# w_out split by column halves and projected during mLSTM's last chunks, x in two transfers a block, the first feed-forward sums beside the projection

## Chip, cores and metric

One core of one Trainium2 chip. The metric is the device time of one execution in microseconds (us), the median of several runs. The profile is of one execution; its times are counted from the start of its span.

## What is computed

One layer of a bidirectional encoder over two groups of positions (2048 and 256, 2304 in all, width 1024), in float32. An mLSTM head group and an attention head group work on the same normed input, their outputs are projected by `w_out` and added to x, and a feed-forward part with a depthwise convolution of width 3 follows.

```python
h = rmsnorm(x, norm1_w); p = h @ w_in
m_out = mlstm_mixer(mq, mk, mv, mo, gates, b_gates, mh_norm_w)      # 8 heads of 64, both directions
a_out = attention_mixer(aq, ak, av, q_norm_w, k_norm_w)             # 8 heads, 2 key/value heads, no mask
x = x + jnp.concatenate([m_out, a_out], axis=-1) @ w_out            # (2304,1024) @ (1024,1024)
h = rmsnorm(x, norm2_w)
u = centred_dwconv(h @ w_up, conv_w, conv_b); a, g = jnp.split(u, 2, axis=-1)
x = x + (jax.nn.silu(g) * a) @ w_down
y = rmsnorm(x, final_norm_w)
```

## The kernel before

Every float32 product is made of three matmuls in a faster format: each operand is split into a rounded high part (ScalarE, ACT, a copy) and the rest (VectorE, DVE, a subtraction), and high x high, high x low and low x high are added up in PSUM. `split` (L109 to L117) loads a piece of a weight into a staging tile and splits it; `loads` in `phase_c` does the same with the mixed heads.

The stages are: phase A (first norm, attention's projections, gates), then mLSTM and attention together, then the projection by `w_out` (`phase_c`), then the feed-forward part (`phase_d`).

mLSTM goes in four pairs of heads over 9 blocks of 256 positions and 18 chunks of 128; in the last pair `proj_qo` makes a block's queries and gates just ahead of its chunks (`out_steps`). A chunk runs through stages in steps (`out_a`, `out_b`, `out_c`, `out_n`, `out_d`), and `out_d` writes it to `mix_d` (L937). Attention goes in 36 head blocks: for each, the row maxima are found first (px, L574, and its reduction on DVE, L575), then for eight pairs of key tiles scores (ps, L600 and L601), two exponentials on ACT (L604, L605), a subtraction on DVE (pl, L606) and six matmuls by the values (pv, L618). The division at the end of a head block takes four reciprocals (L635), and GpSimd (POOL) multiplies and stores into `mix_d`.

Two generators, one for mLSTM and one for attention, yield estimated costs in us, and `run_both` (L1490 and following) decides whose next step is emitted: mLSTM's count `dm` over its total `nm` is held at 1.3 times attention's share. mLSTM's chunk steps carry a high priority (`MPRI`). When mLSTM's generator ends, its pools are closed, `phase_c` is opened, and from there the order of instructions on TensorE (PE) is that of the program (`manual_schedule`), while the other engines and DMA queues are ordered by a planner that simulates times. Now attention's steps alternate with those of `phase_c`: each attention step adds its cost times `pace` to an account, and when the account covers the cost that `phase_c` has yielded, its next step is emitted. A step with a need also waits until that block of attention's output has been emitted.

```python
        pace = C_ALL / (g.a_total - da)
        while da is not None:
            while have >= cost and (need is None or need in g.mixed):
                have -= cost
                need, cost = next(c)
```

`phase_c` first loads and splits `w_out` in 16 pieces of 128 rows by 512 columns (`weights`): rows 0 to 511 into the slots of mLSTM's weights (tag `w`, 8 slots, staged through 2 tiles of `m_r`), rows 512 to 1023 into a pool `wo` that opens when mLSTM's pools are closed, staged through the tiles for x. Then come nine blocks of 256 positions, the last two swapped. A block has four column groups z of 256 output columns; z 0 and 1 read columns 0 to 511 of `w_out`, z 2 and 3 the rest. A column group is 48 matmuls (L1043) into one of two PSUM tiles po, with a yield after each 12 (`C_MM`). `post` adds x to it (L1049), stores the sum to `x1_d` (L1050) and squares it (L1052); POOL adds up the squares (L1054). `tail_a` and `tail_b` make the second norm in the next block's first two column groups: `tail_b` scales (L1064) and stores to `n2_d` (L1066). The next block's `loads` are issued at z = 1. x has eight tiles of [128, 2, 256], two blocks' worth, and a block loads it in eight transfers (L1034).

The feed-forward part multiplies by a Strassen-like scheme with sums of quarters of its input. For the first block of 772 positions `n2_sums` loads rows of `n2_d`, makes four differences on POOL (L1146) and stores them to `n2t_d` (L1148); `n2_load` brings the operands in and splits them (L1125 to L1127); `up_start` loads two rows of `w_up` (L1158, L1159), splits them (L1171, L1172) and starts their matmuls (L1175). After attention's end the rest of `phase_c` is emitted with one of these seven pieces (two loads, four sums, one load) behind each step.

## Time and profile before

| | us |
|---|---|
| median of 3 runs | 3461.38 (3457.83 to 3462.74) |
| the profiled execution | 3460.48 |
| its span | 3458.8 |
| PE busy | 3342.0 (97%) |
| DVE busy | 2683.1 (78%) |
| ACT busy | 1931.2 (56%) |
| POOL busy | 1119.7 (32%) |

The page cuts the span into 40 slices of 86.5 us and gives each engine's busy share in tenths, and the clock that TensorE was granted. A group of instructions is shown with its line, engine, operation, out<-in names and shape, its count, busy time and mean length, and after the bar the idle time of its engine just before it with what ended it. In the timeline a row is the start, the length, the engine, the line and the operation, and in brackets the idle time before it. Matmuls overlap in a full stream, so their lengths add up to more than the time they take: the step from one start to the next is what counts. SPq is the queue from which most transfers are issued, in order.

### The profile page before, as it was taken

The numbers are of one execution on the slowest core, as the hardware profiler recorded it, in microseconds if no ns is written. First come the engines' busy times: TensorE is split into PE (matmuls) and PEld (weight loads), VectorE is DVE, ScalarE is ACT, GpSimd is POOL, SyncE is SP. The second block draws the span as 40 slices with busy tenths as digits, with TensorE's granted clock in tenths as the row PEclk, the third lists the DMA queues.
The fourth block names the chain that finished last, engine by engine and source line by source line (L and its number), as shares of the span: only waits on it lengthen the run. The fifth ranks groups of instructions, "written<-read, shape, count | busy, mean of one in ns | idle before, by whom it ended". The sixth has DMA issues, their size and how long they took to land. (4 is left out here: it accounts for less than half of the span.)

```text
span 3458.8 us, 55780 instructions
## 1 busy us (share of the span) xinstructions
PE 3342.0 (97%) x20058; PEld 3101.0 (90%) x20058; DVE 2683.1 (78%) x4654; ACT 1931.2 (56%) x4329; POOL 1119.7 (32%) x1328
## 2 busy tenths in 40 slices
PE   7989999999999999899998999999999999999998
PEld 6778888888888888678898999999999999999998
DVE  6885687787778788866656888888888878878776
ACT  4536666667666766654444544446544446555555
POOL 6653132213333323201135233225333224322222
PEclk9999999999999999899999999999999999999999
DMA  6765343343345445412348223213433123421221
GB/s 221 237 203 156 91 136 94 105 126 99 111 147 152 126 124 155 131 34 90 98 143 292 74 93 102 74 60 129 135 105 105 62 74 123 142 73 57 74 74 50
DMA packets 258501, 404.29 MB, mean 117 GB/s; under 512 B 33552, under 2 KB 158256, under 8 KB 258224
## 3 DMA queue, kind: packets, MB, share of 16 engines
q1 hardware_dynamic: 230320, 358.24, 32.3%
q0 software_dynamic: 11344, 33.04, 3.5%
q10 hardware_dynamic: 16560, 9.44, 0.9%
q8 instruction: 158, 2.59, 0.3%
q14 instruction: 119, 0.97, 0.1%
HBM read 316.73 MB, written 83.90 MB: 116 GB/s over the span
## 5 line engine op out<-in xcount | busy, mean ns | idle before, releaser
L1313 PE MATMUL pd<-act,wd 128*128 128x384 f32 (+1 forms) x3120 | 594.2, 336 | 18.7 <-DVE acc L1315 11.4
L1313 PEld LDWEIGHTS pd<-act,wd 128*128 128x128 f32 x3120 | 541.0, 189 | 27.0 <-DVE acc L1315 16.6
L606 DVE TENSOR_TENSOR pl<-ps,ph 128x512 fp32r<-128x512 f32 x520 | 353.9, 684 | 205.6 <-ACT ps L605 202.0
L604 ACT ACTIVATE ph<-ps 128x512 fp32r<-128x512 f32 x520 | 309.6, 595 | 261.1 <-PE ps L601 255.1
L1175 PE MATMUL pa<-nt,wut 128*128 128x386 f32 (+2 forms) x2376 | 453.8, 339 | 0.0
L1175 PEld LDWEIGHTS pa<-nt,wut 128*128 128x128 f32 x2376 | 421.0, 189 | 0.0
L575 DVE TENSOR_REDUCE mx<-px 128x1 f32<-128x512 f32 (+1 forms) x528 | 345.0, 671 | 62.5 <-PE px L574 60.5
L1269 DVE SCALAR_TENSOR_TENSOR y<-u,cw,y 128x768 f32<-128x768 f32 (+1 forms) x264 | 311.6, 1181 | 36.2 <-ACT y L1262 29.3
L1180 POOL TENSOR_TENSOR tw<-ru 128x512 f32<-128x512 f32 x66 | 96.0, 1454 | 742.9 <-DMA ru<-w_up 603.6
L618 PE MATMUL pv<-ph,v 128*128 128x512 f32 (+1 forms) x1040 | 323.2, 403 | 2.4 <-ACT ph L604 2.0
L605 ACT ACTIVATE ps<-ps 128x512 f32<-128x512 f32 x520 | 310.6, 597 | 0.0
L1315 DVE TENSOR_TENSOR acc<-pd,acc 128x384 f32<-128x384 f32 (+1 forms) x544 | 280.8, 537 | 32.3 <-PE pd L1313 31.3
L1191 ACT ACTIVATE u<-pa 128x386 f32<-128x386 f32 (+2 forms) x264 | 128.3, 486 | 317.8 <-PE pa L1175 315.7
L574 PE MATMUL px<-kk,qq 128*128 128x512 f32 (+1 forms) x528 | 208.4, 420 | 18.5 <-DVE mx L575 13.4
L1043 PEld LDWEIGHTS po<-cmx,wo 128*128 128x128 f32 x1728 | 217.5, 191 | 7.3
L1043 PE MATMUL po<-cmx,wo 128*128 128x256 f32 x1728 | 220.4, 282 | 0.0
L600 PE MATMUL ps<-qq,kk 128*128 128x512 f32 x520 | 216.4, 418 | 2.9 <-DVE mx L575 1.6
L601 PE MATMUL ps<-qm,kl 65*128 65x512 f32 x520 | 207.4, 401 | 1.3 <-ACT qm L591 1.3
L764 PE MATMUL mj<-mn,wm 128*128 128x256 f32 x1296 | 202.8, 288 | 3.3 <-ACT og L778 1.9
L764 PEld LDWEIGHTS mj<-mn,wm 128*128 128x128 f32 x1296 | 187.0, 192 | 20.4 <-ACT og L778 2.0
L774 PEld LDWEIGHTS mv<-wm,mn 128*128 128x128 f32 x1296 | 182.7, 190 | 18.5 <-ACT qb L770 2.5
L774 PE MATMUL mv<-wm,mn 128*128 128x256 f32 x1296 | 196.4, 285 | 1.0 <-ACT qb L770 0.9
(288 smaller groups left out, 7290.2 us busy)
## 6 DMA issues: line engine op xcount, KB each, us to landing
ru<-w_up SPq DMA_DIRECT2D x132, 512.0 KB, 3.3
mn<-n_d SPq DMA_DIRECT2D x216, 256.0 KB, 3.3
rd<-w_down SPq DMA_DIRECT2D x66, 512.0 KB, 3.6
n_d<-n1T SPq DMA_DIRECT2D x18, 1024.0 KB, 5.6
dm<-nm_d POOLq DMA_DIRECT2D x72, 256.0 KB, 4.1
mjn<-n_d SPq DMA_DIRECT2D x72, 256.0 KB, 3.2
mvn<-n_d SPq DMA_DIRECT2D x72, 256.0 KB, 3.2
q_d<-qz SPq DMA_DIRECT2D x18, 512.0 KB, 3.4
```

The source lines that it names most:

```text
L575: nc.vector.tensor_reduce(s.mx[:, t, z0:z0 + 1], ps[:, 0:w], AX.X, ALU.max)
L604: nc.scalar.activation(ph, ps, AF.Exp)
L605: nc.scalar.activation(ps, ps, AF.Exp)
L606: nc.vector.tensor_tensor(pl, ps, f32(ph), ALU.subtract)
L618: nc.tensor.matmul(s.pv[0:HD if k in (1, 3) else P, 0:N], v, p, start=(kp == 0 and k == 0), stop=(2 * kp + 2 == s.nk and k == 5))
L764: nc.tensor.matmul(pj[:, o], s.w[c][:, a, o * P:(o + 1) * P], nT[c][:, :, h, :], start=(c + o + k == 0), stop=(c == NCC - 1 and k == 2 and ...
L774: nc.tensor.matmul(pv[:, o], nT[c][:, o, a, :], s.w[c][:, h, 256:512], start=(c + o + k == 0), stop=(c == NCC - 1 and k == 2 and o == 1))
L1043: nc.tensor.matmul(po[:, o], wo[c][z // 2][:, a, n], mx[c][:, h, :], start=(c == 0 and k == 0), stop=(c == NCC - 1 and k == 2))
L1175: nc.tensor.matmul(p, w[:, aa, c, :], ops[k][:, c, bb, 0:n], start=c == 0 and i == 0 and not add, stop=c == NCC // 2 - 1 and i == 2, skip_ ...
L1269: nc.vector.scalar_tensor_tensor(y[:, s:e], u[:, s + k:e + k], cw[:, k, jj:jj + 1], y[:, s:e], ALU.mult, ALU.add)
L1313: nc.tensor.matmul(po, wds[j][c // 4][:, aa, c % 4 * P:(c % 4 + 1) * P], acts[j][:, bb, z0:z1], start=(j == 0 and k == 0), stop=(j == len( ...
L1315: nc.vector.tensor_tensor(accs[c][:, z0:z1], po, accs[c][:, z0:z1], ALU.add)
```

## The change

The pieces of `w_out` are taken by column halves: the eight pieces of columns 0 to 511 go into mLSTM's weight slots, the eight of columns 512 to 1023 into the pool `wo`, staged four at a time through two tiles that have the size of a block of x and its tag. All 16 are emitted at once, without yields between them, and the block of the first `loads` is no longer waited for. One lead of 12 stands for the two of 6 and the eight steps of 0.8. In `run_both`, mLSTM's steps are emitted without attention's between them once its count has passed `nm` less 16 (`M_END`). `C_ALL` goes from 178 to 172, and attention's maxima are spread over one pair more of the head block before (`MXZ` 2 to 1).

x is one tile for a block, with two such tiles, loaded in two transfers; the sums are stored in two transfers a block and the normed block in two.

The four `n2_sums` of the first feed-forward block follow `post` in the sixth block of the projection, with tiles of `phase_c`'s pool (tag `rn`, 2 tiles). After attention's end the first two rows of `w_up` are loaded ahead of everything (`up_load`), and the three `n2_load` pieces follow the first three steps.

```diff
-CX = 8
-NPC = 1
-WSTEP = 2
-CSTEP = 1
-C_W = 0.8
-C_LEAD = 6.0
-C_ALL = 178.0
-MXZ = 2
-TP = 4
+C_LEAD = 12.0
+C_ALL = 172.0
+M_END = 16
+MXZ = 1
...
-    def weights(c):
-        wo.append([wps[c // 4].tile([P, 2, 512], F32R, tag="w", name=f"wo{c}_{k}", bufs=WB) for k in range(2)])
-        for k, w in enumerate(wo[c]):
-            if c < 4:
-                t = g.raw.tile([P, 512], F32, tag="raw", name=f"ro{c}_{k}", bufs=2)
-            else:
-                t = sp.tile([P, 512], F32, tag="x", name=f"ro{c}_{k}", bufs=CX)
-            split(g, w[:, 0, :], w[:, 1, :], g.w_out[0, c * P:c * P + P, 512 * k:512 * k + 512], t)
+    def weights(k, c):
+        w = wps[k].tile([P, 2, 512], F32R, tag="w", name=f"wo{c}_{k}", bufs=WB)
+        wo[k].append(w)
+        if k == 0:
+            t = g.raw.tile([P, 512], F32, tag="raw", name=f"ro{c}_{k}", bufs=2)
+        else:
+            if c % 4 == 0:
+                stage.append(sp.tile([P, 4, 512], F32, tag="x", name=f"ro{c}_{k}", bufs=2))
+            t = stage[-1][:, c % 4]
+        split(g, w[:, 0, :], w[:, 1, :], g.w_out[0, c * P:c * P + P, 512 * k:512 * k + 512], t)
...
-        x = [sp.tile([P, 2, BT], F32, tag="x", name=f"cx{b}_{z}", bufs=CX) for z in range(4)]
+        x = sp.tile([P, NCC, BT], F32, tag="x", name=f"cx{b}", bufs=2)
...
-        for z in range(4):
-            for t in range(2):
-                nc.sync.dma_start(x[z][:, :, t * P:(t + 1) * P], g.xT[2 * b + t, :, 2 * z:2 * z + 2])
+        for t in range(2):
+            nc.sync.dma_start(x[:, :, t * P:(t + 1) * P], g.xT[2 * b + t])
...
-        nc.vector.tensor_tensor(x[z], po, x[z], ALU.add)
-        g.st.dma_start(g.x1_d[b, :, 2 * z:2 * z + 2], x[z])
+        xz = x[:, 2 * z:2 * z + 2]
+        nc.vector.tensor_tensor(xz, po, xz, ALU.add)
+        if z % 2:
+            g.st.dma_start(g.x1_d[b, :, 2 * z - 2:2 * z + 2], x[:, 2 * z - 2:2 * z + 2])
...
+            if z % 4 == 3:
+                g.st.dma_start(g.n2_d[:, z - 3:z + 1, b * BT:(b + 1) * BT], x[:, z - 3:z + 1])
...
-    for c in range(NCC):
-        weights(c)
-        yield None, C_W
+    for k in range(2):
+        for c in range(NCC):
+            weights(k, c)
+    sums = list(range(NCC // 2))
     order = (*range(NB - 2), NB - 1, NB - 2)
-    yield 0, C_LEAD
     nxt = loads(0, 0)
     yield None, C_LEAD
...
             post(b, z, x, po, acc)
+            if n > 4 and sums:
+                n2_sums(g, sp, 0, sums.pop(0), tag="rn", bufs=2)
...
-            todo = [lambda c=c: n2_sums(g, s1, 0, c) for c in range(NCC // 2)]
-            todo[TP:TP] = [lambda k=k: n2_load(g, ops, 0, k) for k in EARLY[:2]]
-            todo += [lambda: n2_load(g, ops, 0, EARLY[2])]
+            rs = up_load(g, s1, 0, NFC)
+            todo = [lambda k=k: n2_load(g, ops, 0, k) for k in EARLY]
             for _ in rest:
-                if todo and g.normed >= {t // BT for t in range(DT[1])}:
-                    for f in todo[0:NPC]:
-                        f()
-                    todo = todo[NPC:]
+                if todo:
+                    todo.pop(0)()
...
-            if da is None or dm * g.a_total < LEAD * da * nm:
+            if da is None or dm > nm - M_END or dm * g.a_total < LEAD * da * nm:
```

More of the change, by code (lines that the diff above doesn't have):

```diff
@@ L1004, in phase_c @@
     nc = g.nc
-    wo = []
+    wo = ([], [])
+    stage = []
     g.normed = set()
-    def weights(c):
-        wo.append([wps[c // 4].tile([P, 2, 512], F32R, tag="w", name=f"wo{c}_{k}", bufs=WB) for k in range(2)])
-        for k, w in enumerate(wo[c]):
-            if c < 4:
-                t = g.raw.tile([P, 512], F32, tag="raw", name=f"ro{c}_{k}", bufs=2)
-            else:
-                t = sp.tile([P, 512], F32, tag="x", name=f"ro{c}_{k}", bufs=CX)
-            split(g, w[:, 0, :], w[:, 1, :], g.w_out[0, c * P:c * P + P, 512 * k:512 * k + 512], t)
+    def weights(k, c):
[8 more added lines that the diff above has]
+        split(g, w[:, 0, :], w[:, 1, :], g.w_out[0, c * P:c * P + P, 512 * k:512 * k + 512], t)
     def loads(n, b):
         mx = []
-        x = [sp.tile([P, 2, BT], F32, tag="x", name=f"cx{b}_{z}", bufs=CX) for z in range(4)]
+        x = sp.tile([P, NCC, BT], F32, tag="x", name=f"cx{b}", bufs=2)
         for z in range(4):
@@ L1042, in mm @@
                 for k, (a, h) in enumerate(((0, 0), (0, 1), (1, 0))):
-                    nc.tensor.matmul(po[:, o], wo[c][z // 2][:, a, n], mx[c][:, h, :],
+                    nc.tensor.matmul(po[:, o], wo[z // 2][c][:, a, n], mx[c][:, h, :],
                                      start=(c == 0 and k == 0), stop=(c == NCC - 1 and k == 2))
@@ L1061, in tail_b @@
         r = rstd_rows(g, ps, r, BT)
-        for z in range(4):
-            for o in range(2):
-                nc.vector.scalar_tensor_tensor(x[z][:, o], x[z][:, o], g.n2w[:, 2 * z + o:2 * z + o + 1],
-                                               r, ALU.mult, ALU.mult)
-            g.st.dma_start(g.n2_d[:, 2 * z:2 * z + 2, b * BT:(b + 1) * BT], x[z])
+        for z in range(NCC):
+            nc.vector.scalar_tensor_tensor(x[:, z], x[:, z], g.n2w[:, z:z + 1], r, ALU.mult, ALU.mult)
+            if z % 4 == 3:
+                g.st.dma_start(g.n2_d[:, z - 3:z + 1, b * BT:(b + 1) * BT], x[:, z - 3:z + 1])
         g.normed.add(b)
-    for c in range(NCC):
-        weights(c)
-        yield None, C_W
+    for k in range(2):
+        for c in range(NCC):
+            weights(k, c)
+    sums = list(range(NCC // 2))
     order = (*range(NB - 2), NB - 1, NB - 2)
-    yield 0, C_LEAD
     nxt = loads(0, 0)
@@ L1131, with n2_sums @@
 SUMS = {"t1": (0, 0), "t3": (0, 1), "t4": (1, 0), "t2": (1, 1)}
-def n2_sums(g, pool, b, c, engs=("gpsimd",) * 4):
+def n2_sums(g, pool, b, c, engs=("gpsimd",) * 4, tag="raw", bufs=RW):
     nc = g.nc
@@ L1140, in n2_sums @@
     for k in range(2):
-        r = pool.tile([P, D], F32, tag="raw", name=f"rn{b}_{c}_{k}", bufs=RW)[:, 0:2 * n].rearrange("p (h t) -> p h t", h=2)
+        r = pool.tile([P, D if tag == "raw" else 2 * NH], F32, tag=tag, name=f"rn{b}_{c}_{k}", bufs=bufs)[:, 0:2 * n]
+        r = r.rearrange("p (h t) -> p h t", h=2)
         nc.sync.dma_start(r, g.n2_d[:, c + NCC // 2 * k, DT[b]:DT[b + 1]].rearrange("p (h t) -> p h t", h=2))
@@ L1148, in n2_sums, with up_load, up_start @@
         g.st.dma_start(g.n2t_d[b, k, :, c, :, 0:n], rs[k])
-def up_start(g, s1, ps, ops, b, jj):
+def up_load(g, s1, b, jj):
+    rs = [s1.tile([P, D], F32, tag="raw", name=f"ru{b}_{jj + k}", bufs=RW) for k in range(2)]
+    for k, r in enumerate(rs):
+        g.nc.sync.dma_start(r, g.w_up[jj + k].rearrange("p c n -> p (c n)"))
+    return rs
+def up_start(g, s1, ps, ops, b, jj, rs=None):
     nc = g.nc
@@ L1156, in up_start @@
     nm = f"{b}_{jj}"
-    r1, r2 = (s1.tile([P, D], F32, tag="raw", name=f"ru{b}_{jj + k}", bufs=RW) for k in range(2))
-    nc.sync.dma_start(r1, g.w_up[jj].rearrange("p c n -> p (c n)"))
-    nc.sync.dma_start(r2, g.w_up[jj + 1].rearrange("p c n -> p (c n)"))
+    r1, r2 = rs or up_load(g, s1, b, jj)
     h = D // 2
@@ L1469, in body @@
             ops = n2_ops(s1, 0, EARLY)
-            todo = [lambda c=c: n2_sums(g, s1, 0, c) for c in range(NCC // 2)]
-            todo[TP:TP] = [lambda k=k: n2_load(g, ops, 0, k) for k in EARLY[:2]]
-            todo += [lambda: n2_load(g, ops, 0, EARLY[2])]
+            rs = up_load(g, s1, 0, NFC)
+            todo = [lambda k=k: n2_load(g, ops, 0, k) for k in EARLY]
             for _ in rest:
-                if todo and g.normed >= {t // BT for t in range(DT[1])}:
-                    for f in todo[0:NPC]:
-                        f()
-                    todo = todo[NPC:]
+                if todo:
+                    todo.pop(0)()
             for f in todo:
                 f()
-            first = [up_start(g, s1, pd, ops, 0, NFC)]
+            first = [up_start(g, s1, pd, ops, 0, NFC, rs)]
             g.c_end()
```

2 lines of the change are left out of this document (1 added, 1 removed).

## The prediction

> **What bounds the kernel now.** I read the page first, then the busy time by stretches around the end of mLSTM, then the groups of TensorE instructions in these stretches, then the timeline. Page, parts 1 and 2:
> ```profile
> span 3458.8 us, 55780 instructions
> PE 3342.0 (97%) x20058; PEld 3101.0 (90%) x20058; DVE 2683.1 (78%) x4654; ACT 1931.2 (56%) x4329; POOL 1119.7 (32%) x1328
> PE   7989999999999999899998999999999999999998
> PEclk9999999999999999899999999999999999999999
> ```
> TensorE (PE) is nearly always busy, so only stretches where it starves can give time back. Two of the dips are slice 17 (1384 to 1470 us) and slice 22 (1816 to 1902): the end of mLSTM and the step into the feed-forward part, which are the places of this change. By stretches (the columns are start:end, length, busy us and instructions of PE, PEld, DVE, ACT, POOL, then the granted clock, DMA share, GB/s):
> ```profile
> 1401.00:1447.00 46.00, 37.95 (x152) 28.06 (x152) 39.84 (x106) 23.64 (x67) 8.04 (x17) 0.74 0.14 46
> 1447.00:1508.00 61.00, 49.63 (x174) 30.66 (x173) 51.58 (x85) 41.54 (x84) 5.10 (x6) 0.89 0.34 101
> 1508.00:1784.00 276.00, 267.38 (x1736) 237.00 (x1735) 169.06 (x294) 131.81 (x262) 41.81 (x42) 0.99 0.27 85
> 1784.00:1872.00 88.00, 81.17 (x645) 80.46 (x645) 53.85 (x77) 26.59 (x49) 48.47 (x42) 0.96 0.78 255
> 1872.00:1912.00 40.00, 37.62 (x205) 36.69 (x204) 35.74 (x43) 26.03 (x45) 22.99 (x15) 0.96 0.74 256
> ```
> In the first two rows DVE is 85 to 87% busy and PE runs few matmuls at a lowered clock: mLSTM is ending and attention alone can't feed PE. Projection starts at 1508, and from there PE is fed until 1784, where attention ends. Between 1784 and 1872 projection runs alone with DMA at 0.78.
>
> To see what PE lost, I need the time of a matmul in a full stream, from four rows of the timeline of PE:
> ```profile
> 1508.02 1.59 PE L1043 MATMUL po<-cmx,wo 128*128 128x256 f32 x12
> ...
> 1509.91 1.08 PE L618 MATMUL pv<-ph,v 128*128 128x512 f32 x4
> 1510.83 0.63 PE L618 MATMUL pv<-pl,v 128*128 128x512 f32 x2
> ...
> 1521.14 3.03 PE L1043 MATMUL po<-cmx,wo 128*128 128x256 f32 x24
> 1524.02 0.39 PE L600 MATMUL ps<-qq,kk 128*128 128x512 f32 x1
> ```
> From start to start, 24 projection matmuls take 2.88 us, 0.12 each (a group of 12 is 1.43), and four attention matmuls 0.92, 0.23 each. The groups of PE, first in 1401 to 1447 (one row), then in 1447 to 1508, then in 1508 to 1784:
> ```profile
> L600 PE MATMUL ps<-qq,kk 128*128 128x512 f32 x14 | 6.4, 468 | 0.4 <-DVE pl L606 0.4
> ```
> ```profile
> L618 PE MATMUL pv<-ph,v 128*64 128x512 f32 (+1 forms) x51 | 16.5, 439 | 1.5 <-ACT ph L604 1.5
> L574 PE MATMUL px<-kk,qq 128*128 128x512 f32 x28 | 13.0, 507 | 6.2 <-DVE mx L575 5.6 <-DVE pl L606 0.4
> L600 PE MATMUL ps<-qq,kk 128*128 128x512 f32 x28 | 12.8, 457 | 2.4 <-DVE mx L575 1.6 <-DVE pl L606 0.7
> L601 PE MATMUL ps<-qm,kl 65*128 65x512 f32 x28 | 11.6, 413 | 0.0
> L618 PE MATMUL pv<-pl,v 128*128 128x512 f32 x26 | 10.2, 431 | 0.0
> ```
> ```profile
> L1043 PE MATMUL po<-cmx,wo 128*128 128x256 f32 x1143 | 149.8, 282 | 0.0
> L618 PE MATMUL pv<-ph,v 128*128 128x512 f32 (+1 forms) x184 | 51.1, 400 | 0.0
> L600 PE MATMUL ps<-qq,kk 128*128 128x512 f32 x86 | 34.6, 402 | 0.0
> L601 PE MATMUL ps<-qm,kl 65*128 65x512 f32 x87 | 34.5, 396 | 0.0
> L618 PE MATMUL pv<-pl,v 128*128 128x512 f32 x92 | 29.1, 398 | 0.0
> L574 PE MATMUL px<-kk,qq 128*128 128x512 f32 x68 | 23.5, 415 | 8.6 <-DVE mx L575 5.0 <-DVE pl L606 3.7
> ```
> 1447 to 1508: 161 x 0.23 + 13 small ones x 0.12 = 38.6 us of work in 61: 22.4 lost. 1508 to 1784: 1143 x 0.12 + 517 x 0.23 + 76 x 0.12 = 265.2 in 276: 10.8 lost, 3.9%.
>
> **The change, part by part.** *Start of projection.* PE's order after the end of mLSTM is the program's, so it can be worked out from the pacing loop. Before, mLSTM's last step comes at 601.0 of attention's 755.4 cost units, the pace is 178 / 154.4 = 1.15, and 18.4 units of weights and lead come first: following the loop, the first projection group stands where 86 of L600 are left. The trace says the same (x86 after 1508), so I trust the loop. After, mLSTM's count passes 590.8 - 16 at 565.1 of attention, everything left of mLSTM (its count really ends at 609.8) is emitted there, the pace is 172 / 190.4 = 0.90 and the lead 12: the first group stands where 114 of L600 are left, the ninth (first of the second column half) at 104, and 24 groups are done at 86. In the trace of before, 114 are left at 1447: 86 + 28. So the change puts 24 x 1.43 = 34.3 us of projection into the stretch that lost 22.4. PE then needs 38.6 + 34.3 = 72.9 us for it, if fed, instead of 61 + 34.3: the gain is 22.4 at most. The stretch 1401 to 1447 stays as it is, since no projection stands in it.
>
> What DVE makes of it: the stretch held 51.6 us of DVE work; 24 groups are 1.5 blocks, and a block's own DVE work, by tile, is:
> ```profile
> L1030 DVE TENSOR_TENSOR cmx<-cmx x72: 404/416/2567, 1398.2 to 1830.0; 128x256 fp32r<-128x256 f32 x72
> ```
> ```profile
> L1064 DVE SCALAR_TENSOR_TENSOR cx<-cx,nw,rs_c x72: 468/475/482, 1568.6 to 1885.9; 128x256 f32<-128x256 f32 x72
> L1049 DVE TENSOR_TENSOR cx<-po,cx x36: 620/691/693, 1517.3 to 1870.5; 128x512 f32<-128x512 f32 x36
> ```
> 8 x 0.42 + 4 x 0.69 + 8 x 0.48 = 10 us, so 15 more at most: 66.6 of 72.9. DVE fits, barely, and PE will still wait sometimes. For the loss that stays I take the 3.9% of the next stretch (2.8 us) and one wait behind a run of reciprocals, as here (timeline of PE, and the stretch around it):
> ```profile
> 1702.96 0.80 PE L574 MATMUL px<-kk,qq 128*128 128x512 f32 x1 [3.31 <-DVE mx L575]
> ```
> ```profile
> 1697.00:1722.00 25.00, 21.47 (x120) 18.59 (x119) 17.94 (x32) 9.47 (x20) 5.33 (x6) 0.86 0.27 82
> ```
> The wait is 3.3 and the clock of 0.86 over 25 us costs another 3.5. So 9.6 stays and **12.8 is gained** (bounds: 0, if DVE sets the pace as it does now, and 22.4). The Trainium skill, page "TensorE: Matmul & The Clock Gate", section "Part 1: The HAM clock gate", gives half rate until some 3.4 us of sustained work have passed. By that such a wait would cost an estimated 1.7 us of clock and not 3.5, and the sum would be 1.8 us lower; the row is this kernel's own, and I keep 3.5.
>
> *Weights by column halves.* The splits are the same 16 (ACT and DVE, two of each 512 columns). Only the first half must be in before projection starts, in slots that the last mLSTM projection frees. The second half needs the pool that opens when mLSTM has ended, by DVE's and SP's timelines:
> ```profile
> 1447.29 0.28 DVE L936 TENSOR_TENSOR mmx<-mT,ogT 128x128 f32<-128x128 f32 x1
> ...
> 1467.08 0.67 DVE L115 TENSOR_TENSOR wo<-ro,wo 128x512 fp32r<-128x512 f32 x1
> ```
> ```profile
> 1451.69 2.24 SPq L112 DMA_DIRECT2D ro<-w_out  x5
> ...
> 1463.06 5.60 SPq L1034 DMA_DIRECT2D cx<-xT  x10
> ```
> mLSTM's last write is at 1447.3, just when the first group is due; its PSUM banks pass to projection then. The last eight splits are done at 1467.8. The ninth group comes 10 of the stretch's 28 L600 and 8 groups after 1447: 10/28 of 61 us and 11.4 us, at about 1480. Cost 0 as long as that order holds; the price if not is the last rival's.
>
> *x in two transfers.* A block issues 2 loads for 8, 2 stores of x for 4 and 2 of the normed block for 4: 10 issues fewer on SP, some 0.3 to 0.5 us each, off the path. A block's x is now freed and loaded as a whole; a larger load lands later (issues by line, KB each, median us to landing):
> ```profile
> cx<-xT SPq DMA_DIRECT2D x72, 128.0 KB, 3.3
> ...
> rn<-n_d SPq DMA_DIRECT2D x8, 386.0 KB, 5.5
> ```
> It is asked for at a block's second column group and used at the end of the next block's first, four groups of 12 x 4 matmuls later (23 us even when projection runs alone). Cost 0; without that cover it would be the 2.2 us between the two rows, a block, 20 in all.
>
> *First sums beside the projection.* Eight loads and eight stores of 386 KB (6.2 MB) and 16 POOL operations leave the stretch after 1784 and go beside block 5, and the first w_up rows are asked for at once. In 1784 to 1872 PE shows:
> ```profile
> L1043 PE MATMUL po<-cmx,wo 128*128 128x256 f32 x587 | 71.0, 282 | 0.0
> L1175 PE MATMUL pa<-n,wu 128*128 128x386 f32 x12 | 4.4, 538 | 6.2 <-ACT wu L1171 6.2
> ```
> The one large wait, 6.2, is for a split of w_up whose load came late in a full DMA stretch. With 6.2 of the 88 x 255 = 22.4 MB gone and the load first in the queue it goes: **6.2 gained** (bounds: 0, and 6.2 plus the 2.4 idle of 1872 to 1912). Next late is the last n2 load, with DVE at 36 of 40 us after 1872, which stays. After attention 43 groups are left instead of 49, 61 us, so the other 16.2 MB have 61 us where all took 88; at full use (255 / 0.78 = 327 GB/s) they need 50, so this cover is thin.
>
> Sum: the profiled execution took 3460.5 (span 3458.8 and 1.7 around it), less 12.8 and 6.2 is 3441.5; the median is 0.9 above it: **3442**.
>
> **The rivals.** *DVE keeps the pace* until 1520: 3 us instead of 12.8, 3452. For it: PE's waits in 1447 to 1508 are for DVE; against it, DVE has 9.4 us free there. *More is filled*: all 22.4, 8.6 at the step and some 4 us of the 46 in 1401 to 1447, if projection gets ahead of mLSTM's last chunks: 3426. *POOL holds up DVE*: POOL's sums next to attention. In 1784 to 1872 they are:
> ```profile
> L1146 POOL TENSOR_TENSOR rn<-rn,rn 128x386 f32<-128x386 f32 x8 | 9.0, 1130 | 2.8 <-DMA rn<-n_d 2.6
> ```
> Sixteen of these, 18 us, would all have to stop DVE with PE behind it: 3460, no change. Against it: DVE is idle in 107 of the 276 us of the stretch that takes them. The Trainium skill, page "SBUF — State Buffer", section "SBUF: two separate sides", has this rule: a GpSimd operation and a DVE operation with two SBUF inputs lock each other out for a whole instruction. The 2567 ns maximum of L1030 would agree with it, its 416 median says that it is rare.
>
> *mLSTM's last chunks hold attention back*: PE's written order now begins at 124 of L600, and 10 of the 14 of 1401 to 1447 come after that point, while mLSTM is still at work. If those instructions can't pass mLSTM's, these 10 L600 with the rest of their five pairs (60 matmuls of 0.23), 14 us, come late: 3456, no change.
>
> *Slower*: PE's order stops at the ninth group. It needs a third PSUM bank pair, so the first x, which now waits for a staging tile of w_out's second half (x has two buffers, both taken by that stage). Before, the x transfers went out by 1468.7. PE comes to the ninth group at about 1480; each us that x lands later than that stops attention too. From 1499 on the gain of 19 is used up; an x that lands only at 1510, after both stages and behind other transfers, gives 3472. Against it: the first stage's four splits should be done by about 1460.
>
> **How the numbers follow.** As forecast 0.50 (own range 3433 to 3450), DVE keeps the pace 0.16, more is filled 0.16, POOL 0.04, attention held back 0.06, slower 0.08. A measurement here can tell 0.2%, 7 us, so faster is below 3454.5: 0.82; the two no-change cases 0.10; slower 0.08. The range 3422 to 3458 leaves out the slower case and the ends of the others.
>
> **What would show it.** Right: the first L1043 near 1450, 24 groups of it before 86 of L600 are left, PE with over 115 matmuls in 20 us from 1460 on, the clock back at 1.00, no 6.2 us wait for wu, L1146 of block 0 before attention ends. Wrong: PE waits before L1043 for wo, cx or a PSUM bank, or L574's waits for DVE as long as now.

## The result, and the profile after

| | before | after |
|---|---|---|
| median of 4 runs each, us | 3459.61 (3456.51 to 3462.74) | 3429.99 (3423.08 to 3432.66) |
| ratio after / before | | 0.9911, 95% interval 0.9893 to 0.9929 |
| the profiled execution, us | 3460.48 | 3428.88 |

The change saves 30 us. The profiled execution lies 1.1 us below its median. The page of the changed kernel, parts 1 and 2:

```profile
span 3427.2 us, 55596 instructions
PE 3329.3 (97%) x20058; PEld 3098.4 (90%) x20058; DVE 2677.3 (78%) x4654; ACT 1931.2 (56%) x4329; POOL 1120.9 (33%) x1328
PE   7989999999999999899999999999999999999998
PEclk9999999999999999999999999999999999999999
```

The dip of PE in slice 22, the step into the feed-forward part, is gone (the one in slice 17 stays), and the clock row has no 8 left. The share of PE is still 97%: the page alone would not show what happened. The stretches do (same columns as in the prediction's table):

```profile
1393.00:1445.00 52.00, 42.47 (x197) 31.41 (x196) 48.30 (x122) 30.34 (x80) 10.47 (x20) 0.87 0.25 74
1445.00:1524.00 79.00, 76.91 (x468) 66.12 (x468) 60.46 (x104) 46.79 (x95) 11.55 (x12) 0.98 0.37 112
1524.00:1768.00 244.00, 240.46 (x1517) 211.20 (x1516) 165.51 (x288) 129.12 (x256) 52.34 (x55) 0.99 0.34 111
1768.00:1848.00 80.00, 78.15 (x611) 77.31 (x610) 48.00 (x78) 30.99 (x54) 40.37 (x30) 1.00 0.76 257
```

The second row runs from 114 of the scores L600 left (now L595) to 86 left. Before, it had 204 matmuls in 65 us at a clock of 0.89; now 468 in 79 us at 0.98. Lines of the changed code are lower by a few numbers: L600 is L595, L606 is L601, L574 and L575 are L569 and L570, L936 is L931, L1043 is L1041, L1049 is L1048, L1146 is L1149, L1175 is L1184. PE's timeline where projection starts:

```profile
1438.91 0.39 PE L596 MATMUL ps<-qm,kl 65*128 65x512 f32 x1
1439.42 0.33 PE L926 MATMUL mT<-ident,hh 128*128 128x128 f32 x1
1440.13 1.70 PE L1041 MATMUL po<-cmx,wo 128*128 128x256 f32 x12 [0.38 <-DVE mmx L931]
1441.66 0.63 PE L569 MATMUL px<-kk,qq 128*128 128x512 f32 x2
1442.12 1.08 PE L613 MATMUL pv<-ph,v 128*128 128x512 f32 x4
1443.04 0.63 PE L613 MATMUL pv<-pl,v 128*128 128x512 f32 x2
1443.51 1.60 PE L1041 MATMUL po<-cmx,wo 128*128 128x256 f32 x12
```

The first projection group comes 68 us earlier than before (1508.02). It follows mLSTM's last transposition at once and waits 0.38 us for mLSTM's last write, whose PSUM bank it takes over. From there a group of 12 stands between every few attention matmuls. DVE's and SP's timelines around it, the first with mLSTM's last write and the last splits of `w_out`'s second half, the second with the loads that follow:

```profile
1439.79 0.29 DVE L931 TENSOR_TENSOR mmx<-mT,ogT 128x128 f32<-128x128 f32 x1 [0.42 <-PE mT L926]
...
1451.28 1.29 DVE L110 TENSOR_TENSOR wo<-ro,wo 128x512 fp32r<-128x512 f32 x2 [0.45 <-ACT wo L108]
```

```profile
1440.51 3.93 SPq L107 DMA_DIRECT2D ro<-w_out  x8
1444.69 4.28 SPq L1027 DMA_DIRECT2D cmx<-mix_d  x6
1449.36 1.34 SPq L1032 DMA_DIRECT2D cx<-xT  x2
```

The eight pieces of the second half go out together as soon as the pool opens, and x behind them at 1449. The first half had been split by 1409.1.

To add up PE's losses I use one measure for all kernels of this study: the length of a stretch, less the matmuls in it times their step in a full stream (0.234 us for 512 columns, 0.119 for 256, 0.177 for 386; small ones 0.11). The result is time in which PE waited or ran at a lower clock. The columns are bounded by events of the program, not by times: the last `proj_qo` matmul, 114, 86 and 40 score matmuls left, attention's end, and the 84th and 252nd matmul of w_up (all of L1184's). The two columns from attention's end to the 252nd together are called the step.

```
us that PE lost    qo-114  114-86  86-40  40-end  end-84th  84th-252nd  later   sum
before               22.1    22.0    5.7     5.4      13.8         1.2   25.2  95.4
after                19.7     4.6    5.3     0.5       3.0         2.2   30.5  65.8
after, run again     20.0     5.9    4.0    -0.2       2.7         2.6   26.8  61.8
```

Nearly all of the gain is in three places: 17 us in 114-86, 6 us from there to attention's end, 10 us at the step (from 15.0 to 5.2 and 5.3). The two profiles of the changed kernel differ by 4 us, nearly all of it late in the feed-forward part, so little is read into less than that in a single profile.

### The profile page after: what moved, and what is told of

Its sections match the earlier page's. It is cut to its first block, busy times and chain, and to the rows that moved or that the text cites. A ratio compares the mean times of both kernels' runs of the same rounds, so it can differ in the third digit from the quotient of the medians.

```text
span 3427.2 us, 55596 instructions
## 1 busy us (share of the span) xinstructions
PE 3329.3 (97%) x20058; PEld 3098.4 (90%) x20058; DVE 2677.3 (78%) x4654; ACT 1931.2 (56%) x4329; POOL 1120.9 (33%) x1328
## 5 line engine op out<-in xcount | busy, mean ns | idle before, releaser
L601 DVE TENSOR_TENSOR pl<-ps,ph 128x512 fp32r<-128x512 f32 x520 | 352.7, 683 | 181.5 <-ACT ps L600 173.4
L1184 PE MATMUL pa<-nt,wut 128*128 128x386 f32 (+2 forms) x2376 | 454.3, 339 | 0.0
L1184 PEld LDWEIGHTS pa<-nt,wut 128*128 128x128 f32 x2376 | 421.6, 190 | 0.3 <-ACT u L1200 0.3
L570 DVE TENSOR_REDUCE mx<-px 128x1 f32<-128x512 f32 (+1 forms) x528 | 345.5, 670 | 74.4 <-PE px L569 72.4
L1189 POOL TENSOR_TENSOR tw<-ru 128x512 f32<-128x512 f32 x66 | 94.1, 1425 | 732.5 <-DMA ru<-w_up 558.5
L600 ACT ACTIVATE ps<-ps 128x512 f32<-128x512 f32 x520 | 310.3, 597 | 0.0
L1041 PEld LDWEIGHTS po<-cmx,wo 128*128 128x128 f32 x1728 | 220.7, 191 | 8.2 <-DVE mmx L931 0.6
L1041 PE MATMUL po<-cmx,wo 128*128 128x256 f32 x1728 | 224.2, 284 | 0.4 <-DVE mmx L931 0.4
L595 PE MATMUL ps<-qq,kk 128*128 128x512 f32 x520 | 215.5, 416 | 4.2 <-DVE mx L570 2.4
L569 PE MATMUL px<-kk,qq 128*128 128x512 f32 (+1 forms) x528 | 202.8, 413 | 6.0 <-DVE mx L570 2.9
```

The source lines that it names most:

```text
L570: nc.vector.tensor_reduce(s.mx[:, t, z0:z0 + 1], ps[:, 0:w], AX.X, ALU.max)
L600: nc.scalar.activation(ps, ps, AF.Exp)
L601: nc.vector.tensor_tensor(pl, ps, f32(ph), ALU.subtract)
L1041: nc.tensor.matmul(po[:, o], wo[z // 2][c][:, a, n], mx[c][:, h, :], start=(c == 0 and k == 0), stop=(c == NCC - 1 and k == 2))
L1184: nc.tensor.matmul(p, w[:, aa, c, :], ops[k][:, c, bb, 0:n], start=c == 0 and i == 0 and not add, stop=c == NCC // 2 - 1 and i == 2, skip_ ...
```

## The experiments

All of them were timed beside the kernel before on the same chip. Ratios are against that kernel, so "dearer by" (than the changed kernel timed again, 0.9913) is the difference of two ratios times 3456 us; each ratio has about 0.0013 either way, so two kernels under 6 us apart are not told apart by their times alone, and then only the traces speak. The losses of PE, by the columns above:

```
us that PE lost    qo-114  114-86  86-40  40-end  end-84th  84th-252nd  later   sum
start at 86 left     18.7    19.4   -0.4     1.0      12.0         2.3   23.6  76.6
mLSTM not finished   20.5    17.6    5.5     1.5      12.2         2.6   25.1  85.0
start at 124 left    29.6     0.1    1.4     3.7       3.4         2.6   27.2  68.0
maxima over 6 pairs  23.2     8.0   10.7     3.1       4.5         2.1   25.9  77.5
w_out by rows        25.2     4.0    3.3    -0.2       2.5         4.6   25.8  65.2
x in 8 transfers     19.8     5.4    4.1     1.0       5.4         4.3   25.9  65.9
sums after attention 19.4     3.7    2.6    -0.4       9.5         1.1   24.3  60.2
same, w_up first     19.5     3.7    3.4    -0.3      18.5         3.0   28.0  75.8
low parts on POOL    20.5     5.8    4.6     0.3       3.7         2.6   28.0  65.5
maxima over 8 pairs  19.9     5.2    2.9     2.5       8.2         2.1   28.6  69.4
before, 7 pairs      22.0    21.4    2.7     3.9       6.2         6.6   25.2  88.0
```

**The changed kernel again**, as the base.

> The changed kernel as it is, timed again beside the others. Theory: 3430 us, 30 below the kernel before; the matmuls of attention, mLSTM, projection and w_up between 1440 and 1880 lose about 15 us less PE time in the stretch after mLSTM, 5 in the late overlap and 9 at the step into the feed-forward part. If the fourth part of this (some 4 us lost again in the feed-forward part, at 2300 to 2600) was chance, the time is rather 3426.

3425.64 us, ratio 0.9913 (0.9899 to 0.9926).

**Projection starts as late as before.**

```diff
-C_LEAD = 12.0
-C_ALL = 172.0
+C_LEAD = 59.0
+C_ALL = 215.0
```

> The changed kernel with the projection started as late as before: the lead is 59 instead of 12 and the pace 215 instead of 172, so that the first group stands where 86 of the score matmuls L600 are left (24 groups fewer by then), and some 95 groups are done at attention's end. Halves, transfers of x and the early sums stay. Theory (the gain of the stretch after mLSTM is the 24 groups put into it): 18 to 22 us slower than the changed kernel, about 3449, with 22 us of PE time lost in that stretch again. Rival (the weights by halves, the fewer transfers or the sums bring most of the gain): within 8 us of the changed kernel, below 3438.

3443.11 us, 0.9959 (0.9947 to 0.9972): 16 us dearer than the changed kernel beside it. The first group stands at 1498.32, and 114-86 loses 19.4, nearly as much as before the change (22.0). So the early start is what fills this stretch. The step gets worse with it and loses 14.3 instead of 5.3: when attention's last scores are done, 648 of the 1728 projection matmuls are left instead of 552, and the sums, which follow the sixth block, end later too (their last operation starts at 1779.9 instead of 1757.2). That this is why the step is dearer is argued; shown is where PE waits there, for DVE's adding of x:

```profile
PE po L1041 <- DVE cx L1048: 6.1, 3, 4.6
```

**mLSTM's last steps not emitted ahead of attention's.**

```diff
-M_END = 16
+M_END = -100
```

> The changed kernel without the new rule for mLSTM's last steps: they alternate with attention to their end as before (M_END out of reach), so that the written order starts at 100 of L600 instead of 124; pace and lead constants as changed, the first projection group is then due at 90 of L600, with 4 groups done at 86 instead of 24. Halves, x and sums stay as changed. Theory (what counts is how many groups stand in the stretch after mLSTM): nearly as slow as the kernel with the late lead, 13 to 18 us above the changed kernel, about 3440, first group near 1485 to 1495 us. Rival (the halves by themselves let projection start early, the rule for the last steps adds little): within 6 us of the changed kernel.

3447.44 us, 0.9970 (0.9959 to 0.9982): 20 us dearer. `dm` never passes `nm` + 100, so mLSTM's last steps alternate with attention's as before the change, and `phase_c` opens later: the first group stands at 90 left, 1494.92, 114-86 loses 17.6 again, and the step 14.8. Of the two numbers that set the start, `M_END` is the one that opens `phase_c` early; by the loop, without it the written order would begin at 100 left, so that no lead could put the first group at 114.

**Projection starts at 124 left.**

```diff
-C_LEAD = 12.0
+C_LEAD = 1.0
```

> The changed kernel with a lead of 1 instead of 12: the first group is due at 124 of L600, about 1420 us in the changed kernel's time, 20 us before mLSTM's last write, and 31 groups instead of 24 are done at 86. Theory (the first group can't start before mLSTM's last PSUM bank is free, and PE's order is fixed, so attention stands behind it): PE waits at the first group for the last mmx, some 10 to 20 us; 3 to 12 us slower than the changed kernel. Rival (that wait costs nothing, because DVE sets the pace there and catches up meanwhile, or the bank comes earlier): within 3 us or faster.

3433.95 us, 0.9933 (0.9920 to 0.9945): 7 us dearer. PE's waits from 1393 to 1465 in this kernel, then from 1393 to 1445 in the changed one (columns: us in total, times, longest):

```profile
PE mN L901 <- DVE dn L906: 3.4, 1, 3.4
PE mN L901 <- DVE mmx L931: 3.3, 1, 3.3
PE mT L926 <- DVE hh L919: 3.2, 3, 1.9
```

```profile
PE mN L901 <- DVE mmx L931: 3.1, 1, 3.1
PE px L569 <- DVE mx L570: 1.7, 3, 0.8
```

The first group needs a PSUM bank of mLSTM's, so PE's order here runs through mLSTM's last chunks with less attention between them, and PE waits for their DVE steps (dn and hh, 6.6 us that the changed kernel doesn't have). This is like the rival "mLSTM's last chunks hold attention back" in small, and a lead of 12 stays clear of it. Filling earlier only moves the loss: 114-86 loses nothing now, and the stretch ahead of it loses 10 us more.

**Maxima over six pairs of the head block before, as before the change.**

```diff
-MXZ = 1
+MXZ = 2
```

> The changed kernel with attention's maxima spread as before (MXZ 2), which sets the last maxima of a head block one pair of key tiles earlier and puts three of them in a pair more often. First group still due at 114 of L600, 100 groups done at attention's end. Theory: the 5 us less lost in the late overlap come from the even spread, since PE's waits there were for these reductions and those behind them on DVE: 4 to 6 us slower than the changed kernel, with PE waits for L570 in 1658 to 1768. Rival (they come from the longer time that projection has been ahead, or are chance): within 3 us.

3440.76 us, 0.9956 (0.9943 to 0.9969): 15 us dearer, three times what was expected. PE's waits of px from 1440 to 1780 in the kernel before, in the changed one and in this one:

```profile
PE px L574 <- DVE mx L575: 10.6, 10, 3.3
PE px L574 <- DVE pl L606: 4.0, 4, 1.6
```

```profile
PE px L569 <- DVE pl L601: 1.1, 1, 1.1
PE px L569 <- DVE mx L570: 1.0, 3, 0.5
```

```profile
PE px L569 <- DVE mx L570: 11.2, 10, 3.1
PE px L569 <- DVE pl L601: 4.7, 4, 2.5
```

In the changed kernel the waits of px for DVE's reduction come and go with this one number: 16 maxima a head block in six pairs are three behind each of the first four, in seven pairs three behind the first two and two behind the rest. (That holds from where mLSTM's steps are all emitted, 124 left here and 100 left before the change. Ahead of it, by another constant, four stand behind each of the first four pairs.) px takes its PSUM tiles from the same pool as the scores (tag `sc`, four tiles), and DVE has to empty each by a reduction of 0.68 us, between subtractions of as much; where three px stand in a row, PE stops at the one that finds no tile, and everything behind it in PE's order stops too. PE's timeline bears this out: of the 16.0 us that px waits here from 1440 to 1780, 13.5 are at the third px between two pairs of scores (11 waits in 24 such rows of three), and none at the 13 rows of two. That the third finds no tile is argued from the program.

**The kernel before with seven pairs**, and nothing else changed.

> The kernel before with one number changed: attention's maxima spread over one pair more (MXZ 1). Theory: the spreading stands on its own feet. In the kernel before PE waits 10.6 us for mx and 4.0 us for pl at L574 in 1440 to 1780, in the changed kernel 1.0 and 1.1 at the same place, and with MXZ back at 2 in the changed kernel 11.2 and 4.7 again. So the kernel before gains about what the changed one lost, 8 to 15 us: ratio 0.9955 to 0.9975, and its own px waits for mx after 1440 fall below 4 us. Rival: the spreading pays only where projection fills PE's queue early; in the kernel before DVE sets the pace between 1400 and 1508 whatever the order of its work, and the gain stays under 5 us (ratio above 0.9985).

3447.42 us, 0.9975 (0.9966 to 0.9983): 8.6 us faster than the kernel before, but not by the way the theory said. Over 1380 to 1780 px still waits 9.9 us for mx (13.4 in the kernel before), most of it ahead of 1512:

```profile
PE px L574 <- DVE mx L575: 9.9, 9, 3.1
PE ps L600 <- DVE mx L575: 2.0, 2, 1.5
```

After 1512, where projection stands between the pairs, they fell to one of 1.8 us from 5.0; 114-86 lost 21.4 as ever. But this run can't say what the spreading does there: the number counts only from 100 left, 1480.9 here, and the longest wait, 3.1 us at 1464, stands ahead of that, in a row of four. The kernel with the late start can: its maxima stand in seven pairs from 124 left on, and 114-86 lost 19.4 all the same. So without projection in it that stretch is hardly helped by the spreading; that the spreading pays because projection gives PE other work between two px is argued. The profiled run here lay 4.6 us above its median, so the size of its step is not read.

**Maxima over all eight pairs.**

```diff
-MXZ = 1
+MXZ = 0
```

> The changed kernel with the maxima spread evenly over all eight pairs (MXZ 0, two behind each pair). Theory: nothing is left to gain there, since PE waits only 1.0 us for mx and 1.1 us for pl at L569 in 1440 to 1780: within 4 us of the changed kernel. Rival A: the last maximum now stands in the last pair, so its transposition and the row m4r that the next head block's first scores read come late; PE would wait one to two us at each of some 14 head blocks, 10 to 25 us slower, seen as waits of pr or ps for m4r. Rival B: DVE's queue gets smoother again in 1397 to 1440, where PE loses 20 us, and it is 5 us or more faster.

3429.60 us, 0.9928 (0.9916 to 0.9940): 5 us dearer by the ratios, within what the times can tell. PE's waits from 1524 on for m4r and qm are 0.7 and 0.5 us, so rival A is not seen, nor is B (19.9 in qo-114). The step loses 10.3 instead of 5.3, with 2.8 us of one wait for POOL's rcol_c; whether that is the edit or chance stays open.

**Pieces of w_out by rows, as before the change.**

```diff
-        w = wps[k].tile(...)
-        if k == 0:
+        w = wps[c // 4].tile(...)
+        if c < 4:
...
-            if c % 4 == 0:
+            if k == 0 and c % 2 == 0:
...
-    for k in range(2):
-        for c in range(NCC):
+    for c in range(NCC):
+        for k in range(2):
```

> The changed kernel with w_out taken by rows as before (both column halves of rows 0 to 511 into mLSTM's slots, rows 512 to 1023 staged through the two tiles of x), everything else as changed. The first group, due at about 1440 us, now needs the last rows, which can only be loaded once mLSTM has ended. Theory (the early start needs the halves): PE stops before the first group until about 1455 to 1465 and attention with it; 10 to 20 us slower than the changed kernel, 3440 to 3450. Rival (loading the second part is quick enough, so the order of the pieces doesn't matter): within 4 us, and no wait of more than 3 us before the first group.

3431.42 us, 0.9930 (0.9917 to 0.9944): 6 us dearer, less than the theory's 10 and at the edge of what the times can tell. Waits of PE, and of its weight loads, from 1439 to 1452:

```profile
PE po L1041 <- ACT wo L108: 2.2, 4, 0.7
PE po L1041 <- DVE wo L110: 0.5, 2, 0.2
```

```profile
PEld po L1041 <- ACT wo L108: 3.3, 4, 1.1
PEld po L1041 <- DVE wo L110: 1.3, 4, 0.4
```

By rows, the first column group needs rows 512 to 1023 as well, which can only be staged once mLSTM's pools close. PE follows their splits one by one for some 5 us (25.2 in qo-114), until they are done by 1450. By halves, the first groups find all that they need, and this wait of about 5 us is what the trace shows the halves to be worth.

**x in eight transfers a block, the sums in four stores, the normed block in four**, with x still one tile.

```diff
-        for t in range(2):
-            nc.sync.dma_start(x[:, :, t * P:(t + 1) * P], g.xT[2 * b + t])
+        for z in range(4):
+            for t in range(2):
+                nc.sync.dma_start(x[:, 2 * z:2 * z + 2, t * P:(t + 1) * P], g.xT[2 * b + t, :, 2 * z:2 * z + 2])
...
-        if z % 2:
-            g.st.dma_start(g.x1_d[...], x[:, 2 * z - 2:2 * z + 2])
+        g.st.dma_start(g.x1_d[...], xz)
...
-            if z % 4 == 3:
-                g.st.dma_start(g.n2_d[...], x[:, z - 3:z + 1])
+            if z % 2:
+                g.st.dma_start(g.n2_d[...], x[:, z - 1:z + 1])
```

> The changed kernel with x loaded in eight transfers of 128 KB again, x1 stored in four and the normed block in four; the tiles stay as changed (one tile a block). Theory: these transfers are hidden, within 3 us of the changed kernel. Rival (the 5 us less lost in the late overlap, from 40 of L600 to attention's end, come from fewer transfers on SP's queue): 4 to 6 us slower, with that stretch losing 5 us again.

3432.46 us, 0.9928 (0.9916 to 0.9941): 5 us dearer by the ratios, more than expected, but with intervals that touch. The trace puts 4 of them at the step (9.7 instead of 5.3), where its longest wait is one of 2.3 us for ACT, which reads a feed-forward product (u). The mechanism is not shown.

**The sums, the n2 loads and the w_up loads in their old place**, after attention's end.

```diff
-            if n > 4 and sums:
-                n2_sums(g, sp, 0, sums.pop(0), tag="rn", bufs=2)
...
-            rs = up_load(g, s1, 0, NFC)
-            todo = [lambda k=k: n2_load(g, ops, 0, k) for k in EARLY]
+            rs = None
+            todo = [lambda c=c: n2_sums(g, s1, 0, c) for c in range(NCC // 2)]
+            todo[4:4] = [lambda k=k: n2_load(g, ops, 0, k) for k in EARLY[:2]]
+            todo += [lambda: n2_load(g, ops, 0, EARLY[2])]
...
-                if todo:
+                if todo and g.normed >= {t // BT for t in range(DT[1])}:
```

> The changed kernel with the first sums, the first n2 loads and the first w_up loads back in their old place and order behind attention's end; early projection, halves and transfers of x stay. Theory: the 9 us gained at the step come from there, so 8 to 11 us slower than the changed kernel, about 3440, with DMA near its full share and a wait of some 6 us for w_up again. Rival (the step gained because projection ended in another state, or because x is moved in fewer transfers): less than 4 us slower.

3428.66 us, 0.9922 (0.9908 to 0.9935): 3 us dearer, which the times can't tell from nothing. The step itself does get worse, by 5 us in the trace (10.6), with these waits from 1780 to 1920, and DVE's timeline ahead of the first of them:

```profile
PE rs_c L131 <- POOL cacc L1057: 5.5, 1, 5.5
PE pb L1181 <- DVE wu L1178: 1.6, 1, 1.6
```

```profile
1833.52 3.46 DVE L1371 TENSOR_TENSOR wd<-rd,wd 128x512 fp32r<-128x512 f32 x2
1836.90 0.68 DVE L1048 TENSOR_TENSOR cx<-po,cx 128x512 f32<-128x512 f32 x1
```

The wait for w_up is 1.6 us, not 6.2, even with the loads in their old place; that it shrinks because the projection, filled early, leaves less behind attention's end is argued. In its stead PE waits, from 1835.62 to 1841.16, for the last block's squares. POOL adds those up (cacc), but the first block's sums were through on POOL at 1810.4: the squares are late because DVE adds x to the last column group only at 1836.90, behind two splits of w_down. In the changed kernel it does so at 1830.65, as soon as PE is done with the group. Having these pieces early takes 5 us from the step in this trace, then, by the order in which the queues stand; what the sums cost in their new place is weighed below.

**The same, with the first two rows of w_up loaded ahead of everything.**

```diff
-            rs = None
+            rs = up_load(g, s1, 0, NFC)
```

> The changed kernel with the sums and the n2 loads back after attention's end, as in the version with everything of that part in its old place (3 us slower than the changed kernel), but with the first two rows of w_up loaded ahead of everything. Theory: what the step lost was the late w_up; loaded first, the step loses about 4 us instead of 9.5, the cheaper stretches before it stay, and the time is 1 to 5 us below the changed kernel's. Rival: the sums' own transfers after attention's end make the n2 operands late, whatever w_up does, and it stays 2 to 5 us slower than the changed kernel.

3443.72 us, 0.9969 (0.9957 to 0.9981): 19 us dearer, 14 more than any theory had. PE's longest wait at the step, then DVE's behind it, then SP's queue, and what SP's queue itself waited for from 1800 to 1826:

```profile
PE po L1041 <- DVE cx L1048: 9.4, 1, 9.4
```

```profile
DVE cx L1048 <- DMA cx<-xT: 8.2, 1, 8.2
```

```profile
1816.00 2.37 SPq L1065 DMA_DIRECT2D n_d<-cx  x2
...
1822.59 3.30 SPq L1032 DMA_DIRECT2D cx<-xT  x2
```

```profile
SPq L1148 <- POOL rn L1146: 9.5, 5, 4.4
```

The x of the last block went out at 1822.59; in the changed kernel it goes out at 1806.50 and lands in time for PE, though DVE waits 6.7 us for it there. x has two tiles, so the load waits until the block before last is scaled and stored (L1063, L1065). It was scaled in time here, from 1798.96 (1800.19 in the changed kernel), but its stores went out at 1816.00 instead of 1801.86: they stood in SP's queue behind the sums' loads and stores, and these waited 9.5 us for POOL, which had the first rows of w_up to add up between the sums (L1186 to L1189). PE's written order then stops at the projection group that needs the PSUM tile. What the delayed x does is the mechanism of the rival "slower", at the other end of the projection.

**All low parts of w_out subtracted on POOL.**

```diff
-        split(g, w[:, 0, :], w[:, 1, :], g.w_out[...], t)
+        nc.sync.dma_start(t, g.w_out[...])
+        nc.scalar.activation(w[:, 0, :], t, AF.Copy)
+        nc.gpsimd.tensor_tensor(w[:, 1, :], t, f32(w[:, 0, :]), ALU.subtract)
```

> The changed kernel with the 16 subtractions that make w_out's low parts on POOL instead of DVE. Theory: DVE bounds the stretch 1397 to 1440 (44 us of work in 45 between 1400 and 1445, five of these subtractions, 3.4 us, among it), so PE loses 3 to 8 us less there and the kernel is that much faster. Rival: a subtraction takes over 1.2 us on POOL (a 64x512 product takes 1.28 there), and mLSTM's mr (L100, L101), on which each of its last chunks waits, queues behind it; the chunks end later, the first projection group with them, and the kernel is 3 us or more slower.

3432.21 us, 0.9932 (0.9919 to 0.9944): not faster, 6.6 us dearer by the ratios, with intervals that touch. The subtractions on POOL, PE's longest wait in 1393 to 1445, and one of mLSTM's operations on DVE there, in the changed kernel and in this one:

```profile
L1017 POOL TENSOR_TENSOR wo<-ro,wo 128x512 fp32r<-128x512 f32 x14 | 18.1, 1310 | 12.3 <-ACT wo L1016 12.2
```

```profile
PE mN L901 <- DVE s L892: 4.0, 1, 4.0
```

```profile
L904 DVE SCALAR_TENSOR_TENSOR dn<-s 128x4 f32<-128x4 f32 x5 | 0.8, 152 | 0.0
L904 DVE SCALAR_TENSOR_TENSOR dn<-s 128x4 f32<-128x4 f32 x5 | 2.6, 530 | 0.1
```

qo-114 loses 20.5, no less, but DVE was not relieved. Seven subtractions of 0.68 us, 4.8 us in all, left it in this stretch, and it was busy for 47.80 of 52 us instead of 48.30, since others took longer beside POOL's subtractions: besides dn the splits of cmx (694 ns instead of 418) and mLSTM's s at L907 (573 instead of 414). One dn that starts at 1403.72, as POOL goes into two subtractions (1404.02, 2.61 us), takes 1.59 us. So what a less busy DVE would give PE stays untested. Of the 9.3 us of waits listed for PE in this stretch of the changed kernel, 6.0 are for steps of mLSTM's chain from chunk to chunk, 3.1 of them in one wait (mmx); the granted clock of 0.87 takes another 6.8 of the 52. The chunks didn't end later (the first group stands at 1440.4), so the rival's way isn't seen, and the 6.6 us are not explained.

## Why the prediction was right, and where its terms were off

It said 3442 with a range of 3422 to 3458, and faster; 3430 was measured. That is 3 us below the own range of the forecast case (3433 to 3450), and nearer to the rival "more is filled" (3426): of that rival's three terms the step came about (8.6 said, 10 measured) and half of the 4 us ahead of 114 left, but not the whole of 22.4. By its steps:

- *The start of projection*: the places worked out from the pacing loop held. First group beside mLSTM's last write, at 1440 (it said near 1450); 25 groups before 86 are left (24). The ninth group started at 1470.6 (about 1480), and from 1460 to 1480 PE had 120 matmuls, 114 when run again (over 115). Undoing the start alone cost 16 and 20 us in two ways.
- *What DVE makes of it*: 9.6 us were to stay in this stretch, 4.6 and 5.9 did. The wait of 3.3 us behind reciprocals and its 3.5 us of clock, taken over from the row at 1703, did not come: no wait for mx after 1440 is over 1.5 us in either profile of the changed kernel, the clock is 0.98. So the term gained 17, not 12.8. The 9.6 counted that wait twice, since the 3.9% come from a stretch that holds it, and the wait was read too simply. DVE's timeline of the kernel before:

```profile
1695.28 3.38 DVE L635 RECIPROCAL rs<-rs 64x128 f32<-64x128 f32 x4
1698.59 3.72 DVE L1030 TENSOR_TENSOR cmx<-cmx 128x256 fp32r<-128x256 f32 x4
```

  PE waits from 1699.65 to 1702.96, when the reciprocals are over: it waits behind four splits of cmx that take 3.72 us instead of 1.6, beside operations on POOL (more on this at the sums). Such a wait came back in two other kernels, 3.15 us at 1561.82 with six pairs and 2.81 at 1591.45 with mLSTM's last steps not emitted ahead, and the clock of the 25 us around each was 0.93, 1.7 us lost and not 3.5. The rule of the Trainium skill's page "TensorE: Matmul & The Clock Gate", section "Part 1: The HAM clock gate", agrees with these two rows: by it, 1.7 was estimated. The row at 1703 cost twice that.
- *The maxima over one pair more* are in the diff, and the prediction priced them nowhere. This is the term that it left out without a reason: the kernel with six pairs is 15 us dearer. That kernel gains 15 us on the kernel before, near the 19 that were added up, and loses 8.0 in 114-86, near the 9.6. The prediction had the rows for it: 8.6 us of idle time before L574 in the 1508 to 1784 group, named as a wait for mx and pl, with the reduction's spread the very thing that the number sets. It kept that stretch's loss (10.8) as it was, and 86-40 and 40-end together went from 11.1 to 5.8 and 3.8.
- *Weights by halves* at cost 0: right, the last splits were done at 1452.6 (about 1460 had been said for the first four, 1467.8 read for all eight before the change) and the ninth group came at 1470.6; that the first groups would have waited some 5 us without the halves was not said.
- *x in two transfers* at cost 0: not refuted; eight transfers are about 5 us dearer by the times, within their intervals. But the cover of 23 us isn't there at the end: the last block's x could only be asked for when its tile was free, at 1806.50, and DVE waited 6.7 us for it, until 1814.11. PE didn't wait then; 16 us more delay cost PE 9.4.
- *First sums beside the projection*: 6.2 was the wait for w_up, and that wait is gone. PE's timeline at the step has no idle time in brackets:

```profile
1817.05 13.56 PE L1041 MATMUL po<-cmx,wo 128*128 128x256 f32 x111
1830.45 2.29 PE L1184 MATMUL pa<-n,wu 128*128 128x386 f32 x12
```

  But the edit to which it was put down is not enough. With sums and loads in their old place, the waits for w_up were 1.6 and 0.7, the step lost 5 us more and the whole kernel 3; with the late start 9 of the step's 10 us came back, in two kernels (14.3 and 14.8), though w_up was loaded first in them and PE waited 1.8 and 1.5 us in all for its splits: other waits had taken their place. And in the kernel before with seven pairs, with all loads in their old place, no wait for w_up is over 2.1 us. So the wait of 6.2 was no fixed price of the late load. The step's gain hangs mostly on the early start; that this is because less projection, fewer squares and fewer stores are left behind attention's end is argued. The sums themselves, by what they did (views of tile rn in the changed kernel):

```profile
L1149 POOL TENSOR_TENSOR rn<-rn x8: 862/870/935, 1675.9 to 1757.2; 128x386 f32<-128x386 f32 x8
L1149 POOL TENSOR_TENSOR rn<-rn,rn x8: 863/976/1027, 1682.0 to 1756.2; 128x386 f32<-128x386 f32 x8
```

  Each takes 0.86 to 1.03 us, all in the column 40-end, which lost 0.5 and -0.2 with them and -0.4 and -0.3 without. So the rival by which they stop DVE for 18 us did not come; PE lost at most 1. DVE's own work did get longer beside them, by its groups from 1672 to 1760, in the changed kernel and with the sums after attention:

```profile
L1029 DVE TENSOR_TENSOR cmx<-cmx 128x256 fp32r<-128x256 f32 x14 | 10.1, 752 | 5.0 <-ACT cmx L1028 4.8
```

```profile
L1029 DVE TENSOR_TENSOR cmx<-cmx 128x256 fp32r<-128x256 f32 x16 | 9.1, 599 | 2.9 <-ACT cmx L1028 2.9
```

  That fits the rule on two-input operations that lock each other out, which the prediction took from the Trainium skill's page "SBUF — State Buffer", section "SBUF: two separate sides": 14 operations 0.15 us longer each, 2 us of DVE, in a stretch where DVE has time to spare. Counted one by one it is plainer. In the traces of the 14 kernels here, no split of cmx that met no two-input operation on POOL took over 0.43 us, and each of the 181 of 1008 that took over 0.8 us met one. In the kernel before these are 20 of 72, so they are not as rare as the prediction took them to be, and three of them make the wait at 1703.

So the sum of 19 was 31.6 in the traces (95.4 against 63.8, the mean of the two after). The difference: 4 more from 114-86, 6 from there to attention's end, 4 more from the step, 2 ahead of 114 left, and 3 given back late in the feed-forward part, where the two profiles don't agree. The mechanism of the start was right. The value of the likeliest case lay 12 us high mainly because one edit in the diff was read and not costed; that the rest, the step above all, came out near its term by the road forecast is not shown and was in part luck. The effects don't add up as single edits: start, finish of mLSTM and spreading each cost 15 to 20 of the 30 when undone alone. That fits PE being fed only when projection is there and px doesn't block the queue ahead of it.

No version here beats the changed kernel. Starting earlier, spreading further, moving subtractions to POOL and moving the sums back all came out level or dearer.

## What to carry to other kernels

Where an engine starves at the end of one stage, work out from the program's own pacing where the next stage's first instruction will stand, and what resource it takes over from the old one; that place was right here to a group, and undoing it cost 16 to 20 us, more than undoing a move of transfers did (3 to 6; 19 only where one was half undone). Price every constant in a diff, a spacing number above all: here rows of three px cost PE waits that rows of two did not, and six pairs instead of seven cost the kernel 15 us. When a wait at a later step shrinks, undo the earlier edits one by one before crediting the edit that stands beside it.

## What was not expected of the hardware

That moving work from DVE to POOL need not relieve DVE: seven subtractions, 4.8 us, went, and its busy time fell by 0.5 us, because other operations on it took longer beside POOL's. That the wait of 3.3 us on PE at 1703 came from a row of such stretched splits: a split of cmx takes 0.42 us alone and took up to 1.55, once 2.57, beside POOL in the kernel before. And that 6.2 MB and 16 POOL operations fit beside a stretch in which PE runs at 98% of its time, at 1 us of PE or less.
